# Router on un-normalised sums, narrow projection first, and subtractions moved to VectorE in a one-core encoder block

## The chip, the core and the metric

The kernel runs on one core of a Trainium2 chip. The metric is the device time of one execution in microseconds; less is better. The engines are named as in the profile: PE (TensorE matmuls), PEld (its weight loads), DVE (VectorE), ACT (ScalarE), POOL (GpSimd), SP (SyncE, which here issues most DMAs).

## What is computed

One encoder block over 256 tokens of width 1024, in float32. The parts that matter here:

```python
h @ w_in   # columns: [A: q | c_kv | q_idx | k_idx | w_idx] [B: q | k | v] [gate_A | gate_B]
# mixer A: the indexer's scores choose 64 keys of each query, then latent attention over them
# mixer B: chunked attention with a learned relative bias
m = sigmoid(gate_A) * (y_A @ Wa) + sigmoid(gate_B) * (y_B @ Wb); out = m @ w_out
x = LN(alpha * x + out)                 # ln1: (x - mean) * rstd * g + b
x = LN(alpha * x + MoE(x))              # top-4 of 32 experts of width 1024

def moe_ffn(x, w_router, b_router, ...):
    logits = (xf @ w_router + b_router).astype(jnp.float32)
    top_val, top_idx = lax.top_k(logits, TOP_K)
    gates = jax.nn.softmax(top_val, axis=-1)
    # each of the 32 experts: clamped SwiGLU of its tokens, weights of 3 x 1024 x 1024
```

## The kernel before, in words

All weights are read once. They pass through a pool of 27 SBUF slots of 1 MB (128 x 2048 float32). `load_next` (L85) issues the next weight load on SP's queue as soon as it is called in program order; the load then waits in that queue until the slot that it gets is released by its last reader. `pump(reserve)` issues loads until only `reserve` slots are unpromised; the table `RESERVE` gives the number for each call, and `used()` frees two slots and pumps.

**Mixer.** The tokens (xT, transposed, 256 KB per 256 features) are multiplied by w_in. To get float32 accuracy from a faster matmul form, a 1 MB chunk of weights is split into a rounded half `hi` (ACT, L178) and the rest `lo` = chunk − hi (L183, two subtractions of 128x1024), and three products hi·x_hi, hi·x_lo, lo·x_hi are summed (the tuple `THREE`). `LO_ENGINE` gives for each of 24 chunks the engine of the subtraction, V for DVE and G for POOL; `AHEAD` says how many chunks are split ahead of use. `LO_MERGED` gives the engine of the same subtraction for the merged branches.

PE's order is: index query projection (L244 in plain float32 for three of eight k, L247 split), narrow projection `g0` (L253: index keys, latent, index weights), then eight projections T0 to T7 of 512 columns (`project_T`, L282, and `project(5)`, L267), with small attention steps between: `ktr` (L347, transposes of index key and latent), `kat` (L373), `va` (L377), index scores, scores of mixers B and A. `maxima`, `exps`, `normalise` (L423, DVE) and `turn` (L446: 24 PE transposes of the probabilities `biasB` for mixer B, `sa` for A) and `attend` make each attention. After project(5) comes turn(sB), then T6, attend(vb), T7, turn(sA). Then the branches (L528), the output projection w_out (`out_chunk`, four quarters of the contraction for two token blocks) with the residual in `x1`.

**Norm and router.** `norm_apply` writes z = (x1 − mean)·rstd and x1 = z·g + b on DVE; `turn_z` transposes z, `route_sums` multiplies by the router weights scaled with ln1's gain, `route` picks the four experts, `count_up` and `one_hot` give each expert's row numbers, and `gather` (L651) multiplies x1 by the one-hot matrix so that the rows of the first two experts stand together. Small bf16 matmuls without use (`warm`, L226) stand between the steps.

**Experts.** 32 experts of 12 loads of 1 MB follow: gate and up (L775, L777), down (L809), summed back by L821. The last of them ends the program.

Of the kernel before, what the change touches and what calls it, by code (L numbers as in the profile page):

```python
# [50 lines left out]
def body(nc, tc, slots, sm, psp, xT_d, x_d, w_g0, w_qi, w_in, ikgb_d, wuk_d,  # L51
# [197 lines left out]
    free(6)  # L249
    g0ps = [bank("g0ps") for _ in range(NT)]  # L250
    for k in range(KD):
        for tb in range(NT):
            PE.matmul(g0ps[tb][:, 0:200], xT[:, k, tb * 128:(tb + 1) * 128], g0[:, k, :],  # L253
                      start=(k == 0), stop=(k == KD - 1))
    free(2)
# [113 lines left out]
    for j2 in range(2):  # L369
        p = bank("kat")  # L370
        for jj in range(2):
            j = 2 * j2 + jj
            PE.matmul(p[:, jj * 256:(jj + 1) * 256], wuk[:, j * 128:(j + 1) * 128], ckT, start=True, stop=True)  # L373
        acopy(kaT[:, 2 * j2:2 * j2 + 2, :], p.rearrange("p (j t) -> p j t", j=2))
# [189 lines left out]
    def norm_apply(tb, groups):  # L564

        m, dst = lnmv[:, tb, :], x1[:, tb, :]
# [3 lines left out]
        hs = [slice(i * 512, (i + 1) * 512) for i in range(2)]  # L570
        for cs in hs:
            V.tensor_scalar(z[:, cs], dst[:, cs], m[:, 0:1], m[:, 3:4], op0=ALU.subtract, op1=ALU.mult)
        for cs in hs:
            V.scalar_tensor_tensor(dst[:, cs], dst[:, cs], m[:, 0:1], ln1[0][:, cs], op0=ALU.subtract, op1=ALU.mult)
        for cs in hs:
            V.scalar_tensor_tensor(dst[:, cs], dst[:, cs], m[:, 3:4], ln1[1][:, cs], op0=ALU.mult, op1=ALU.add)
# [11 lines left out]
    def turn_z():  # L588
        for h in range(2):
            p = bank("rtr")  # L590
            for i in range(4):
                k = 4 * h + i
                PE.transpose(p[:, i * 128:(i + 1) * 128], z[:, k * 128:(k + 1) * 128], ident)
            acopy(zT[:, 4 * h:4 * h + 4, :], p.rearrange("p (k t) -> p k t", k=4))
# [3 lines left out]
    def router_row():  # L598
        p = bank("rrow")
        for k in range(KD):  # L600
            PE.matmul(p[0:1, 0:NE], lnc[:, 1, k:k + 1], wr[:, k, :], start=(k == 0), stop=(k == KD - 1))
        V.tensor_tensor(rrow, rrow, p[0:1, 0:NE], op=ALU.add)

    def route_sums(copy=vcopy):
# [8 lines left out]
    def route(tb):

        p = bank("rt")[:, 0:NE]
        PE.matmul(p, ones, rrow, start=True, stop=False)
        PE.matmul(p, rsum, eye4, start=False, stop=True)
        acopy(lg[:, tb, :], p)
        V.max(v8[:, tb, :], p)
# [1 line left out]
        V.match_replace(gt[:, tb, :], v8[:, tb, :], p, LOW)
        V.tensor_tensor(selb[:, tb, :], gt[:, tb, :], p, op=ALU.not_equal)
# [105 lines left out]
    norm_apply(1, 4)
    gather(P[:, 0].rearrange("p e s -> p (e s)"), 128, 0, gps)
    turn_z()  # L730
    route_sums(acopy)
    warm(6)
# [366 lines left out]
```

## Time and profile before

| | |
|---|---|
| device time, median of 3 runs | 1137.94 us (1136.99 to 1138.29) |
| device time of the profiled execution | 1137.62 us |
| span of the profiled execution | 1136.0 us |
| busy in the span: PE, DVE, ACT, POOL | 1061.2, 293.4, 228.7, 96.6 us |
| DMA over the span | 437.52 MB, mean 385 GB/s |

The span is what the trace covers; 1.6 us of the device time lie around it. A busy PE is not PE at its peak. The profiled execution lies 0.3 us under the median.

### The profile page before, as it was taken

The page shows a single profiled execution, that of the slowest core. Times are in us where ns is not written, and L with a number is a line of the kernel's source. Part 1 is how long each engine was busy: PE and PEld are TensorE (multiplying, and loading weights), DVE is VectorE, ACT ScalarE, POOL GpSimd, SP SyncE. Part 2 cuts the span into 40 slices and gives each one's busy share as a digit, 9 for nine tenths or more (in the row PEclk, how much of TensorE's full clock was granted, in tenths as well). Part 3 has the DMA queues.
Part 4 walks back from the last instruction along what each step waited for, and adds up shares of the span by engine and source line. Part 5 has one row for each costly group of instructions (what it writes and reads, how often), then busy time and mean ns, then how long its engine had stood idle before and what let it go on. Part 6 is the DMA issues. An engine that isn't in the chain of part 4 may idle for free. (4 is left out here: it accounts for less than half of the span.)

```text
span 1136.0 us, 13723 instructions
## 1 busy us (share of the span) xinstructions
PE 1061.2 (93%) x5599; PEld 535.3 (47%) x5599; DVE 293.4 (26%) x711; ACT 228.7 (20%) x425; POOL 96.6 (9%) x54
## 2 busy tenths in 40 slices
PE   8998999999999999999999988996999999989985
PEld 8997998543434343434343434342434343333432
DVE  5398556322111111111111111111021102011123
ACT  3557542211111111201111101111111111011112
POOL 4675232000000000000000000000000000000001
PEclk9999999999999999999999999998999999998998
DMA  9925477999999999999999999999999999999994
GB/s 361 419 108 221 149 267 293 404 399 420 421 421 421 422 420 421 420 422 421 420 422 421 421 421 421 421 421 419 421 421 421 422 421 421 421 407 421 421 419 173
DMA packets 63932, 437.52 MB, mean 385 GB/s; under 512 B 7252, under 2 KB 7892, under 8 KB 11892
## 3 DMA queue, kind: packets, MB, share of 16 engines
q1 hardware_dynamic: 62998, 434.20, 92.9%
q10 hardware_dynamic: 864, 2.36, 0.6%
q8 instruction: 47, 0.77, 0.3%
q14 instruction: 23, 0.19, 0.0%
HBM read 435.48 MB, written 1.05 MB: 384 GB/s over the span
## 5 line engine op out<-in xcount | busy, mean ns | idle before, releaser
L777 PE MATMUL gu<-ld,wa 128*64 128x512 f32 x1024 | 460.1, 602 | 28.9 <-DMA ld<-in_dram 28.9
L775 PE MATMUL gu<-ld,wa 128*64 128x512 f32 x1024 | 458.9, 601 | 7.0 <-PEq L851 3.8
L809 PE MATMUL y<-ld,wc 128*64 128x512 f32 x992 | 239.2, 596 | 16.3 <-DMA ld<-in_dram 16.3
L775 PEld LDWEIGHTS gu<-ld,wa 128*64 128x64 f32 x1024 | 135.8, 138 | 226.5 <-issue 219.7
L796 DVE TENSOR_TENSOR wc<-tr,wb 128x256 f32<-128x256 f32 x64 | 27.0, 421 | 706.6 <-PE tr L792 706.6
L777 PEld LDWEIGHTS gu<-ld,wa 128*64 128x64 f32 x1024 | 135.2, 138 | 112.7 <-DMA ld<-in_dram 60.3
L809 PEld LDWEIGHTS y<-ld,wc 128*64 128x64 f32 x992 | 77.0, 136 | 164.6 <-issue 122.2
L178 ACT ACTIVATE wb<-gu 128x512 f32<-128x512 f32 x64 | 38.2, 597 | 445.1 <-PE gu L775 232.9
L178 ACT ACTIVATE wc<-y 64x512 f32<-64x512 f32 (+1 forms) x66 | 38.2, 578 | 224.2 <-PE y L809 216.7
L183 POOL TENSOR_TENSOR lo<-ld,hi 128x1024 fp32r<-128x1024 f32 x30 | 76.5, 2575 | 62.6 <-ACT hi L178 50.3
L984 POOL PARTITION_BROADCAST ln<-ln x1 | 2.3, 2298 | 929.0 <-DMA ld<-in_dram 929.0
L651 PEld LDWEIGHTS ga<-wa,x 128*128 128x128 f32 x512 | 61.6, 196 | 12.3 <-issue 12.2
L651 PE MATMUL ga<-wa,x 128*128 128x128 f32 x512 | 64.8, 285 | 0.0
L282 PE MATMUL fm<-xh,hi 128*128 128x256 f32 x224 | 64.3, 287 | 0.0
L282 PE MATMUL fm<-xl,hi 128*128 128x256 f32 x224 | 63.4, 283 | 0.0
L282 PE MATMUL fm<-xh,lo 128*128 128x256 f32 x224 | 63.4, 283 | 0.0
L821 PE MATMUL sum<-wc,wb 128*128 128x512 f32 x120 | 54.0, 592 | 0.0
L178 ACT ACTIVATE hi<-ld 128x1024 fp32r<-128x1024 f32 x48 | 47.5, 1048 | 26.8 <-PE fm L282 12.3
L282 PEld LDWEIGHTS fm<-xh,hi 128*128 128x128 f32 x224 | 42.9, 192 | 0.7 <-issue 0.4
L282 PEld LDWEIGHTS fm<-xl,hi 128*128 128x128 f32 x224 | 43.0, 192 | 0.2 <-issue 0.2
L282 PEld LDWEIGHTS fm<-xh,lo 128*128 128x128 f32 x224 | 43.0, 192 | 0.0
L798 ACT ACTIVATE wa<-wc 128x256 f32<-128x256 f32 x64 | 26.6, 416 | 79.4 <-DVE wc L797 78.8
(235 smaller groups left out, 828.6 us busy)
## 6 DMA issues: line engine op xcount, KB each, us to landing
ld<-in_dram SPq DMA_DIRECT2D x404, 1024.0 KB, 19.8
ld<-in_dram SPq DMA_DIRECT2D x8, 512.0 KB, 13.7
wq<-in_dram ACTq DMA_DIRECT2D x3, 512.0 KB, 7.8
biasB<-in_dram SPq DMA_DIRECT2D x1, 1024.0 KB, 12.1
x<-in_dram SPq DMA_DIRECT2D x1, 1024.0 KB, 6.8
g<-in_dram SPq DMA_DIRECT2D x1, 800.0 KB
xT<-in_dram SPq DMA_DIRECT2D x3, 256.0 KB, 7.5
out_dram<-acc SPq DMA_DIRECT2D x3, 256.0 KB, 2.0
```

Of the source, the lines that this page charges most:

```text
L178: A.activation(o, i, AF.Copy)
L183: sub.tensor_tensor(lo.bitcast(F32R), t, hi, op=ALU.subtract)
L282: PE.matmul(ps[j // 2][:, j % 2 * 256:j % 2 * 256 + 256], part(i, b, k, 4)[:, j * 128:(j + 1) * 128], xHL[a][:, 4 * c + k, :], start=(c + ...
L651: PE.matmul(ps[j // per][:, (j % per) * n:(j % per + 1) * n], x1_cols(tb, j), Pt, start=(tb == 0 and j % per == 0), stop=(tb == 1), skip_g ...
L775: PE.matmul(ps[n][0:64, :], xe(j), wg(j, cs), start=(j == 0), stop=(j == KD - 1), skip_group_check=True)
L777: PE.matmul(ps[n][64:128, :], xe(j), wu(j, cs), start=(j == 0), stop=(j == KD - 1), skip_group_check=True)
L796: V.tensor_tensor(gg, pv[:, :, 0, :], bg(js), op=ALU.add)
L798: A.activation(sg_, gg, AF.Sigmoid, scale=1.702)
L809: PE.matmul(p[64 * n:64 * n + 64, :], hT[:, j, :], wd(j, slice(n * 512, (n + 1) * 512)), start=(j == 0), stop=(j == KD - 1), skip_group_ch ...
L821: PE.matmul(sums[tb][n], lhsT, rhs, start=start, stop=stop, skip_group_check=True)
L984: G.partition_broadcast(ln2_s, ln2_s[0:1, :])
```

## The change

1. **Start.** The loads come in another order: xT on SP's queue and the narrow weights g0 on ACT's, then the index query's weights wq. PE does the narrow projection first, with DVE splitting xT meanwhile; the index query follows, its `lo` on DVE; `ktr` and `kat` move ahead of T0, the index scores follow T0 directly, and T1 moves behind the top-k selection.
2. **Subtractions.** `LO_ENGINE` has V for all chunks but 5, 6 and 7 (before: 9 V and 15 G); `LO_MERGED` has V for all four.
3. **Order of the mixer.** T6 stands ahead of turn(sB), and attend(vb) behind T7.
4. **Router.** The transposes are of x1 as the residual left it, and the logits are put right afterwards: (x1·W − mean·colsum(W))·rstd + row, where W is the router with ln1's gain. ACT applies mean and rstd to x1 (two activations per block). ln1's gain and offset are applied to the gathered rows (8 activations of 128x128), and to x1 itself by two DVE operations in expert 0, where the slot of ln1 is freed. Of 36 warm matmuls of this stage 12 stay, and the gather of the first block stands in four pieces between the steps of the second.
5. `RESERVE` has 1 in place of 3 at its second place and 3 in place of 2 at its fourteenth.

```diff
-LO_MERGED = "GVGV"
-RESERVE = (4, 3, 3, 3, 4, 5, 3, 3, 3, 1, 3, 3, 3, 2, 3, 1, 2, 4, 3, 1, 5, 1, 1, 1, 0)
+LO_MERGED = "VVVV"
+RESERVE = (4, 1, 3, 3, 4, 5, 3, 3, 3, 1, 3, 3, 3, 3, 3, 1, 2, 4, 3, 1, 5, 1, 1, 1, 0)
-LO_ENGINE = "GVVGGGGGGGGGGVGVGVGVGVVV"
+LO_ENGINE = "VVVVVGGGVVVVVVVVVVVVVVVV"
...
-    for k0, n in ((0, 1), (1, 1), (2, 2), (4, 2), (6, 2)):
+    for k0, n in ((0, 1), (1, 1), (2, 2), (4, 4)):
         SP.dma_start(xT[:, k0:k0 + n, :], xT_d[:, k0:k0 + n, :])
-        A.dma_start(wq[k0 // 4][:, k0 % 4:k0 % 4 + n, :], w_qi[:, k0:k0 + n, :])
-    SP.dma_start(g0, w_g0)
+    for k0, n in ((0, 2), (2, 6)):
+        A.dma_start(g0[:, k0:k0 + n, :], w_g0[:, k0:k0 + n, :])
+    for k0, n in ((0, 2), (2, 2), (4, 4)):
+        SP.dma_start(wq[k0 // 4][:, k0 % 4:k0 % 4 + n, :], w_qi[:, k0:k0 + n, :])
...
     exps(sA, 0)
+    project_T(6, gate_sink(1, 0))
     turn(sB, 1)
     free(2)
-    project_T(6, gate_sink(1, 0))
-    attend(vb, 1)
     normalise(sA, 0)
     project_T(7, gate_sink(1, 1))
     free(2)
+    attend(vb, 1)
     turn(sA, 0)
...
+    def norm_apply(tb):
+
+        m, dst = lnmv[:, tb, :], x1[:, tb, :]
+        for i in range(2):
+            cs = slice(i * 512, (i + 1) * 512)
+            A.activation(dst[:, cs], dst[:, cs], AF.Identity, bias=m[:, 4:5], scale=m[:, 3:4])
...
-        PE.matmul(p, ones, rrow, start=True, stop=False)
-        PE.matmul(p, rsum, eye4, start=False, stop=True)
-        acopy(lg[:, tb, :], p)
-        V.max(v8[:, tb, :], p)
+        PE.matmul(p, rsum, eye4, start=True, stop=True)
+        l, m = lg[:, tb, :], lnmv[:, tb, :]
+        V.scalar_tensor_tensor(l, wsum, m[:, 0:1], p, op0=ALU.mult, op1=ALU.add)
+        V.scalar_tensor_tensor(l, l, m[:, 3:4], rowb, op0=ALU.mult, op1=ALU.add)
+        V.max(v8[:, tb, :], l)
...
+    def gathered_z(ps, dst):
+
+        for j in range(KD):
+            A.activation(dst[:, j, :], ps[j // 4][:, j % 4 * 128:(j % 4 + 1) * 128], AF.Identity,
+                         bias=lnc[:, 1, j:j + 1], scale=lnc[:, 0, j:j + 1])
...
         if e == 0:
+            for gain, op in ((ln1[0], ALU.mult), (ln1[1], ALU.add)):
+                V.tensor_tensor(x1, x1, gain[:, None, :].to_broadcast([128, NT, D]), op=op)
+            free()
             open_work()
```

Three places show what the new order does to the queues. First PE at the start, before (the last index query matmuls, then g0 and T0, whose rows are `fm`):

```order
L247 MATMUL qi<-xl,wqh_145 128x256
L247 MATMUL qi<-xh,wql_147 128x256
L253 MATMUL g0ps<-g_69,xT 128x200 x16
L282 MATMUL fm<-xh,hi 128x256
L282 MATMUL fm<-xl,hi 128x256
```

The same place after:

```order
L255 MATMUL qi<-xl,wqh_143 128x256
L255 MATMUL qi<-xh,wql_145 128x256
L341 MATMUL ktr<-ident,kidxT_ckvT 128x128 x4
L359 MATMUL kat<-kidxT_ckvT,uku 128x256 x4
L284 MATMUL fm<-xh,hi 128x256
L284 MATMUL fm<-xl,hi 128x256
```

The narrow projection is gone from between index query and T0 (it stands at the head), and ktr and kat are there instead. Second, DVE around the division of B's probabilities (`biasB`) by their sums, before:

```order
L183 TENSOR_TENSOR lo<-ld,hi 128x1024 x2
L421 RECIPROCAL sums<-sums 128x16
L423 TENSOR_TENSOR biasB_663<-biasB_663,sums 128x1024
L423 TENSOR_TENSOR biasB_664<-biasB_664,sums 128x2048
L175 COPY pt_1205<-ptr 128x512 x2
```

And after:

```order
L185 TENSOR_TENSOR lo<-ld,hi 128x1024 x4
L423 RECIPROCAL sums<-sums 128x16
L425 TENSOR_TENSOR biasB_553<-biasB_553,sums 128x1024
L425 TENSOR_TENSOR biasB_554<-biasB_554,sums 128x2048
L185 TENSOR_TENSOR lo<-ld,hi 128x1024 x4
L177 COPY pt_1319<-ptr 128x512 x2
```

Two more subtractions stand ahead of the division, and four between it and the copies of the transposed probabilities (`pt`). Third, SP's queue around the output projection and the router, with the semaphores that each load waits for, before:

```order
L85 DMA ld<-in_dram 128x2048 [waits DMAHW4_49,PE_49]
L85 DMA ld<-in_dram 128x2048 [waits DMAHW5_49,PE_49]
L85 DMA ld<-in_dram 128x2048 [waits DMAHW6_49,PE_49]
L85 DMA ld<-in_dram 128x2048 [waits DMAHW7_49,PE_49]
L85 DMA ld<-in_dram 128x2048 [waits DMAHW0_49,Pool_49]
L85 DMA ld<-in_dram 128x2048 [waits DMAHW1_49,PE_49]
L85 DMA ld<-in_dram 128x2048 [waits DMAHW2_49]
L85 DMA ld<-in_dram 128x2048 [waits DVE_49,DMAHW3_49,PE_49,Activation_49]
L85 DMA ld<-in_dram 128x2048 [waits DMAHW4_49,DVE_49,Pool_49]
L899 DMA wb<-in_dram 128x256 [waits DMAHW5_49,PE_49]
```

And after (`wb` is a small load of biases of the first experts):

```order
L85 DMA ld<-in_dram 128x2048 [waits DMAHW6_49]
L85 DMA ld<-in_dram 128x2048 [waits DMAHW7_49,PE_49]
L85 DMA ld<-in_dram 128x2048 [waits DMAHW0_49]
L85 DMA ld<-in_dram 128x2048 [waits DMAHW1_49,PE_49,Activation_49]
L922 DMA wb<-in_dram 128x256 [waits DMAHW2_49,PE_49]
L923 DMA wb<-in_dram 128x256 [waits DMAHW3_49]
L85 DMA ld<-in_dram 128x2048 [waits DMAHW4_49,PE_49]
L85 DMA ld<-in_dram 128x2048 [waits DMAHW5_49,DVE_49,Pool_49]
```

The load that takes the slot of ln1 (the one that waits for DVE and POOL) stood ahead of wb and now stands behind it, since the slot is freed in expert 0.

## Rows read from the trace of the kernel before

**Rows 1.** Stretches: length; busy of PE, PEld, DVE, ACT, POOL; granted clock; DMA; GB/s.

```profile
0.00:6.50 6.50, 4.56 (x34) 4.16 (x35) 1.60 (x8) 0.00 (x0) 1.21 (x8) 1.00 0.65 169
16.30:19.70 3.40, 3.40 (x19) 3.40 (x18) 0.00 (x0) 2.77 (x4) 2.60 (x3) 0.50 1.01 422
57.40:109.40 52.00, 51.99 (x402) 48.31 (x400) 45.49 (x95) 29.93 (x59) 33.34 (x13) 1.00 0.45 176
109.40:119.40 10.00, 4.30 (x25) 3.97 (x25) 8.15 (x5) 8.28 (x35) 4.09 (x2) 0.66 0.00 0
148.00:174.10 26.10, 26.10 (x244) 25.80 (x243) 17.35 (x24) 11.02 (x12) 6.55 (x3) 1.00 0.78 302
174.10:197.20 23.10, 23.10 (x150) 19.42 (x148) 14.48 (x24) 4.82 (x8) 4.04 (x2) 1.00 0.75 288
209.90:232.00 22.10, 22.10 (x99) 8.36 (x100) 5.14 (x21) 5.83 (x9) 0.00 (x0) 1.00 1.00 410
232.00:239.00 7.00, 7.00 (x34) 2.30 (x32) 1.37 (x6) 0.00 (x0) 0.00 (x0) 1.00 0.90 321
239.00:1119.40 880.40, 826.75 (x3868) 336.45 (x3864) 145.76 (x432) 123.54 (x235) 2.30 (x1) 0.99 1.01 419
```

**Rows 2.** Waits of SP's queue in 0 to 300 us (total, times, longest).

```profile
SPq L899 <- PE gu L777: 7.6, 1, 7.6
```

**Rows 3.** PE's timeline, start (start, duration, instruction, count, idle before and its releaser).

```profile
15.33 0.39 PE L247 MATMUL qi<-xh,wql 128*128 128x256 f32 x1 [0.99 <-POOL wql L183]
22.43 5.58 PE L253 MATMUL g0ps<-g,xT 128*128 128x200 f32 x32
27.70 0.42 PE L282 MATMUL fm<-xh,hi 128*128 128x256 f32 x1
39.36 0.60 PE L347 MATMUL ktr<-ident,kidxT_ckvT 128*128 128x128 f32 x4
54.21 1.99 PE L373 MATMUL kat<-kidxT_ckvT,uku 128*128 128x256 f32 x8
56.04 1.88 PE L377 MATMUL va<-uku,kidxT_ckvT 128*128 128x512 f32 x4
```

**Rows 4.** PE's timeline at the two turns.

```profile
111.56 0.79 PE L446 MATMUL ptr<-ident,biasB 128*128 128x128 f32 x4 [2.17 <-DVE biasB L423]
115.89 3.75 PE L446 MATMUL ptr<-ident,biasB 128*128 128x128 f32 x20 [3.54 <-DVE biasB L423]
119.39 0.36 PE L282 MATMUL fm<-xh,hi 128*128 128x256 f32 x1
145.46 0.60 PE L446 MATMUL ptr<-ident,sa_vb 128*128 128x128 f32 x4
148.00 0.36 PE L528 MATMUL br<-y,hi 128*128 128x256 f32 x1
```

**Rows 5.** DVE's timeline.

```profile
20.96 8.24 DVE L183 TENSOR_TENSOR lo<-ld,hi 128x1024 fp32r<-128x1024 f32 x4 [5.27 <-ACT hi L178]
40.00 0.55 DVE L348 TENSOR_SCALAR kidxT_ckvT<-ktr,ikgb 128x256 f32<-128x256 f32 x1 [4.76 <-PE ktr L347]
86.01 3.39 DVE L412 TENSOR_REDUCE mx<-biasB 128x8 f32<-128x1024 f32 x2
89.33 1.69 DVE L481 SCALAR_TENSOR_TENSOR sa_vb<-misc 128x128 f32<-128x128 f32 x8
90.94 2.76 DVE L481 SCALAR_TENSOR_TENSOR sa<-misc 128x256 f32<-128x256 f32 x8
105.59 2.36 DVE L183 TENSOR_TENSOR lo<-ld,hi 128x1024 fp32r<-128x1024 f32 x2 [2.00 <-issue]
108.15 7.48 DVE L423 TENSOR_TENSOR biasB<-biasB,sums 128x1024 f32<-128x1024 f32 x2
```

**Rows 6.** DVE's groups of L423 kept apart by shape (busy, mean ns).

```profile
L423 DVE TENSOR_TENSOR sa<-sa,sums 128x2048 f32<-128x2048 f32 x1 | 2.3, 2284 | 0.0
```

**Rows 7.** POOL's timeline beside the division.

```profile
107.53 5.96 POOL L183 TENSOR_TENSOR lo<-ld,hi 128x1024 fp32r<-128x1024 f32 x2 [9.26 <-ACT hi L178]
```

More of the change, by code (lines that the diff above doesn't have):

```diff
@@ L151, in body @@
     SP.dma_start(uku_s[:, 0:1024], wuk_d)
+    for _ in range(4):
+        load_next()
     wr = sm.tile([128, KD, NE], F32, name="wr")
@@ L233, in body @@
     wqHL = [[t.bitcast(F32R).rearrange("p (k c) -> p k c", k=4) for t in ts] for ts in (wqh, wql)]
+    g0ps = [bank("g0ps") for _ in range(NT)]
+    for k in range(KD):
+        for tb in range(NT):
+            PE.matmul(g0ps[tb][:, 0:200], xT[:, k, tb * 128:(tb + 1) * 128], g0[:, k, :],
+                      start=(k == 0), stop=(k == KD - 1))
+        sl = slice(k * 256, (k + 1) * 256)
+        split(xT_s[:, sl], xh_s[:, sl], xl_s[:, sl], vcopy, V)
+    free(1)
     qp = [bank("qi") for _ in range(4)]
     for k in range(KD):
-        sl = slice(k * 256, (k + 1) * 256)
-        split(xT_s[:, sl], xh_s[:, sl], xl_s[:, sl], vcopy, V)
+        sl = slice(k % 4 * 512, (k % 4 + 1) * 512)
         if k >= QI_NATIVE:
-            sl = slice(k % 4 * 512, (k % 4 + 1) * 512)
-            split(wq_s[k // 4][:, sl], wqh[k // 4][:, sl], wql[k // 4][:, sl])
+            split(wq_s[k // 4][:, sl], wqh[k // 4][:, sl], wql[k // 4][:, sl], sub=V)
         for j in range(4):
@@ L248, in body @@
                           start=False, stop=(k == KD - 1 and b == 1))
[L249 to L255, printed above, removed]
+    free(7)
     V.scalar_tensor_tensor(negd, negd, -1.0, negd, op0=ALU.mult, op1=ALU.min)
@@ L290, in copy_to @@
         return lambda js, p: acopy(dst[:, js, :], p)
-    ahead(AHEAD[0])
-    for j in range(4):
-        vcopy(qiT[:, j, :], qp[j][:, 0:256])
     kT_s = slot("kidxT_ckvT")
@@ L356, in relu_sink @@
         A.activation(rl[tb][:, heads[0]:heads[-1] + 1:2, :], ps, AF.Relu)
-    project_T(1, copy_to(kbT))
+    ahead(1)
+    for j in range(4):
+        (acopy if j % 2 else vcopy)(qiT[:, j, :], qp[j][:, 0:256])
+    for j2 in range(2):
+        p = bank("kat")
+        for jj in range(2):
+            j = 2 * j2 + jj
+            PE.matmul(p[:, jj * 256:(jj + 1) * 256], wuk[:, j * 128:(j + 1) * 128], ckT, start=True, stop=True)
+        acopy(kaT[:, 2 * j2:2 * j2 + 2, :], p.rearrange("p (j t) -> p j t", j=2))
+    qb_s = slot("qb")
+    qbT = qb_s[:, 0:1024].rearrange("p (j t) -> p j t", j=4)
+    kbT = qb_s[:, 1024:2048].rearrange("p (j t) -> p j t", j=4)
+    project_T(0, copy_to(qbT))
     for tb in range(NT):
@@ L368, in body @@
     va = uku_s[:, 1024:2048].rearrange("p (b c) -> p b c", b=2)
[L369 to L374, printed above, removed]
     for sb in range(NT):
@@ L397, in body @@
     SP.dma_start(b0_s[:, 0:1024], relb_d[:, 0:1024])
+    project_T(1, copy_to(kbT))
     project_T(2, copy_to(qaT))
@@ L504, in body @@
     mg = sg[0]
-    ones = sm.tile([1, 128], F32, name="ones")
+    ones = sm.tile([128, 128], F32, name="ones")
     V.memset(ones, 1.0)
@@ L508, in body @@
     V.tensor_tensor(wrg, wr, lnc[:, 0, :, None].to_broadcast([128, KD, NE]), op=ALU.mult)
+    V.tensor_tensor(wr, wr, lnc[:, 1, :, None].to_broadcast([128, KD, NE]), op=ALU.mult)
     eye4 = sm.tile([128, NE], F32, name="eye4")
@@ L562, in norm_stats, with norm_of @@
         V.bn_stats(lnst[:, tb, i, :], src[:, i * n:(i + 1) * n])
-    def norm_apply(tb, groups):
-        m, dst = lnmv[:, tb, :], x1[:, tb, :]
+    def norm_of(tb, groups):
+        m = lnmv[:, tb, :]
         V.bn_aggr(m[:, 0:2], lnst[:, tb, 0:groups])
@@ L569, in norm_apply @@
         V.reciprocal(m[:, 3:4], m[:, 2:3])
[L570 to L576, printed above, removed]
+        V.tensor_scalar(m[:, 4:5], m[:, 0:1], m[:, 3:4], -1.0, op0=ALU.mult, op1=ALU.mult)
+    def norm_apply(tb):
[3 more added lines that the diff above has]
+            A.activation(dst[:, cs], dst[:, cs], AF.Identity, bias=m[:, 4:5], scale=m[:, 3:4])
     lg = sm.tile([128, NT, NE], F32, name="lg")
@@ L586, in body, with turn, router_rows, route_sums @@
     cum = []
[L588 to L594, printed above, removed]
+    def turn(tb, js, copy=acopy):
+        p = bank("rtr")
+        n = len(js)
+        for i, j in enumerate(js):
+            PE.transpose(p[:, i * 128:(i + 1) * 128], x1_cols(tb, j), ident)
+        copy(xT1[:, tb, js[0]:js[0] + n, :], p[:, 0:n * 128].rearrange("p (k t) -> p k t", k=n))
     rsum = sm.tile([128, 128], F32, name="rsum")
-    def router_row():
+    def router_rows():
         p = bank("rrow")
[L600 to L604, printed above, removed]
+        PE.matmul(p[:, 0:2 * NE], ones, rows2, start=True, stop=False, skip_group_check=True)
+        PE.matmul(p[:, NE:2 * NE], ones[0:1, :], rrow, start=False, stop=True, skip_group_check=True)
+        V.tensor_scalar(wsum, p[:, 0:NE], -1.0, None, op0=ALU.mult)
+        vcopy(rowb, p[:, NE:2 * NE])
+    def route_sums(tb, copy=vcopy):
         p = bank("rt")
@@ L608, in route_sums @@
             g = k % 4
-            PE.matmul(p[32 * g:32 * g + 32, 0:128], wrg[:, k, :], zT[:, k, :], start=(k < 4), stop=(k >= 4),
+            PE.matmul(p[32 * g:32 * g + 32, 0:128], wrg[:, k, :], xT1[:, tb, k, :], start=(k < 4), stop=(k >= 4),
                       skip_group_check=True)
@@ L615, in route @@
         p = bank("rt")[:, 0:NE]
[L616 to L619 removed]
+        PE.matmul(p, rsum, eye4, start=True, stop=True)
[3 more added lines that the diff above has]
+        V.max(v8[:, tb, :], l)
         V.memset(v8[:, tb, 4:8], -LOW)
[L621 to L622 removed]
+        V.match_replace(gt[:, tb, :], v8[:, tb, :], l, LOW)
+        V.tensor_tensor(selb[:, tb, :], gt[:, tb, :], l, op=ALU.not_equal)
     def count_up(tb):
@@ L638, in body @@
     identa = wa_s[:, 1792:1920]
+    wsum, rowb, rows2 = wa_s[:, 1920:1952], wa_s[:, 1952:1984], wa_s[:, 1984:2048]
+    for i, w in enumerate((wrg, wr)):
+        V.tensor_reduce(rows2[:, i * NE:(i + 1) * NE], w.rearrange("p k e -> p e k"), axis=AX.X, op=ALU.add)
     def x1_cols(tb, j):
@@ L702, in body @@
     zz_s = slot("z")
-    z = zz_s[:, 0:1024]
-    zT = zz_s[:, 1024:2048].rearrange("p (k t) -> p k t", k=KD)
-    norm_apply(0, 2)
+    xT1 = zz_s.rearrange("p (b k t) -> p b k t", b=NT, k=KD)
+    norm_of(0, 2)
     out_chunk(1, 1)
@@ L708, in body @@
     out_chunk(2, 1, (0,))
+    turn(0, range(0, 4))
     out_chunk(3, 1, (0,))
-    router_row()
-    turn_z()
+    turn(0, range(4, 8))
+    router_rows()
+    norm_apply(0)
     norm_stats(x1[:, 1, :], 1, 0, 256)
@@ L715, in body @@
     out_chunk(2, 1, (1,))
-    route_sums(acopy)
+    route_sums(0, acopy)
     out_chunk(2, 1, (2,))
@@ L719, in body @@
     route(0)
+    turn(1, range(0, 4))
     out_chunk(3, 1, (1,))
@@ L724, in body @@
     out_chunk(3, 1, (2,))
+    turn(1, range(4, 6))
+    P0, P1 = [P[:, tb].rearrange("p e s -> p (e s)") for tb in range(NT)]
+    gather(P0, 128, 0, gps, (0, 1))
+    turn(1, range(6, 8))
     norm_stats(x1[:, 1, :], 1, 3, 256)
@@ L727, in body @@
     free(2)
[L728 to L732, printed above, removed]
+    norm_of(1, 4)
+    gather(P0, 128, 0, gps, (2, 3))
+    route_sums(1)
+    norm_apply(1)
+    gather(P0, 128, 0, gps, (4, 5))
     route(1)
-    free(2)
-    warm(20)
+    free(1)
+    gather(P0, 128, 0, gps, (6, 7))
+    warm(8)
     count_up(1)
-    warm(10)
+    warm(4)
     one_hot(0, 1, cum[1])
+    gather(P1, 128, 1, gps)
+    gathered_z(gps, xg_rows(0, KD))
     for tb in range(NT):
-        acopy(pos[:, tb, :], cum[tb])
-    gather(P[:, 1].rearrange("p e s -> p (e s)"), 128, 1, gps)
-    gathered(gps, 128, xg_rows)
+        vcopy(pos[:, tb, :], cum[tb])
     pump(next(pumps))
@@ L1061 @@
     bias = lambda b: b.reshape(NE, 4, 128, 2).transpose(2, 0, 1, 3).reshape(128, NE, KD)
+    pairs = lambda w: w.reshape(4, 128, 2, -1).transpose(1, 0, 2, 3).reshape(128, KD, -1)
     arrs = [
@@ L1075 @@
         np.concatenate([a["ln1_g"][0], a["ln1_b"][0]])[None, :],
-        np.stack([a["ln1_g"][0].reshape(KD, 128).T, a["ln1_b"][0].reshape(KD, 128).T], axis=1),
-        a["w_router"][0].reshape(KD, 128, NE).transpose(1, 0, 2),
+        np.stack([pairs(a["ln1_g"][0])[:, :, 0], pairs(a["ln1_b"][0])[:, :, 0]], axis=1),
+        pairs(a["w_router"][0]),
         a["b_router"],
```

6 lines of the change are left out of this document (removed).

## The prediction

> **What bounds the kernel now.** I read the table of stretches first [rows 1], because one average over the span mixes two regimes. From 239 us to 1119 us the DMA share is 1.01 at 419 GB/s: the experts wait for weights, and nothing that PE, DVE or ACT save there is worth anything. The stretch 209.90 to 232.00 is full too (1.00). Ahead of that the share is 0.45 (57 to 109 us), 0.00 (109 to 119 us), 0.78 and 0.75: the loads stand still because the 27 slots are full and are released only as PE works through the mixer. PE is busy 52.0 of 52.0, 26.1 of 26.1 and 23.1 of 23.1 us in these stretches, so up to about 200 us the kernel is bound by PE's order, and behind it by the bytes still to come. The link is what the sum below uses: when PE reaches the output projection x us sooner, the loads restart x us sooner, run without a pause, and the end comes x us sooner.
>
> The exception in PE's part is 109.40 to 119.40: PE is busy 4.30 of 10.00 us, and its granted clock falls to 0.66. PE's own timeline names the cause [rows 4]: the transposes of B's probabilities wait 2.17 us and 3.54 us for the division on DVE. The second look was PE's start [rows 3]: waits for a subtraction (0.99 us on POOL), and the clock at 0.50, which is 1.2 GHz, from 16.3 to 19.7 us [rows 1]. Last came SP's queue [rows 2], where one load waits 7.6 us for expert 1's matmuls, and DMA drops to 321 GB/s in 232 to 239 us [rows 1].
>
> **The change part by part.** Costs are of the profiled execution (1137.62 us), 0.3 us under the median.
>
> *The turn of B.* What must happen between the end of project(5) at 109.40 and T6 at 119.39 is 24 transposes. The same 24 for mixer A, whose operand is ready, go from 145.46 to 148.00 [rows 4]: 2.54 us. The rest, 10.00 − 2.54 = 7.46 us, is wait and half clock. With T6 in front, PE has 11.7 us of work (T0, of the same shape, takes 27.70 to 39.36 [rows 3]) while DVE divides. In the time of before, the division must then end by 109.4 + 11.7 = 121.1 us; it ended at 108.15 + 7.48 = 115.6 [rows 5].
>
> But DVE gets more to do ahead of it, so I count its row of work from the maxima of B at 86.01: maxima 3.39, the start of A's scores 1.69 + 2.76 [rows 5], four subtractions at 2.36/2 = 1.18 us (a pair takes 2.36 [rows 5]) 4.7, the additions of A's scores taken as long as their start 4.45, maxima of A 3.4, four subtractions 4.7, the two divisions 2.28 for the large one [rows 6] and half of it for the small one, 3.4. Sum 28.5: the end is at 114.5, 6.6 us ahead of need. The divisions are taken at 2.28 us and not at the 7.48 of before because POOL subtracted just then, 5.96 us for two [rows 7], and after the change it doesn't. If the eight subtractions cost the most that a DVE row shows, 8.24/4 = 2.06 us [rows 5], 7.0 us come on top and PE would wait 0.4 us. So +7.4 gained, bounds 5.7 (the two waits alone) to 7.46. What is late if this cover were gone is attend(vb), but it now stands behind T7, 11.7 us more.
>
> The four subtractions between the division and the copies of the turned probabilities [DVE's order in the change] take 4.7 us; 114.5 + 4.7 = 119.2, still ahead of 121.1.
>
> *The start.* Loads: 169 GB/s in the first 6.50 us [rows 1] are 1.10 MB, then 0.42 MB per us. xT and g0, 1.05 + 0.82 = 1.87 MB, are in at 8.3 us; wq, 2.10 MB more, at 13.4 us. The narrow projection takes 27.70 − 22.43 = 5.27 us for 16 matmuls [rows 3], 0.33 each. Four can run on the first quarter of g0, and twelve from 8.3 on end at 12.3 us. The index query follows: 12 float32 matmuls of 128x256 at the rate of kat, (56.04 − 54.21)/4 = 0.46 us [rows 3], 5.5 us; 60 split ones at T0's rate, 11.66/96 = 0.12 us, 7.3 us; end 25.1. Then ktr 0.6, a wait for DVE to scale index key and latent, two of 0.55 us [rows 5], kat 1.83: T0 starts at 28.6. Before, T0 started at 27.70, with ktr and kat still to do: 27.70 + 0.6 + 1.83 = 30.1. Gain 1.5 us. New in it is that PE, after its first four narrow matmuls, waits for data until 8.3 us; before, the clock fell to half for 3.4 us behind two short waits, which cost 1.7 us of work. Whether it falls again the order cannot tell; I take half such a fall, −0.85, bounds 0 and two falls, −3.4. The subtractions of wq on DVE, five of half the width of the 1.18 us ones, are about 3 us in all, beside 5.5 us of float32 matmuls.
>
> The Trainium skill (TensorE: Matmul & The Clock Gate, "Part 1: The HAM clock gate") has the slow clock as the default state that activity lifts; this agrees with the 0.50 behind PE's early waits, and speaks for a fall here, where PE waits for data.
>
> *Subtractions in the branches and the output projection.* In 148.0 to 197.2 us DVE is busy 17.35 + 14.48 = 31.8 of 49.2 us, and POOL does five operations there [rows 1]. As DVE subtractions these five cost 5 × 1.18 = 5.9 at most, to 37.7 of 49.2: nothing on the path, bound −1.0 for the last chunk, which PE needs at once. Covered by PE's 49.2 us.
>
> *Router.* In the stage from 197 to 210 us the new chain is shorter by DVE's four passes over x1 and four over z, but the first expert waits for nothing of it that sets the end: DMA is full from then on [rows 1], so the gain is 0, bound +3.0. The eight activations of the gathered rows and the two DVE passes over x1 in expert 0 (twice 2048 columns, each like the 2.28 us row [rows 6], some 4.6 us, at most double) lie beside gate and up matmuls.
>
> *SP's queue.* One load that now stands ahead of the biases moves behind expert 0: 1.05 MB less are in when the stage ends, 1.05/0.419 = 2.5 us [rows 1], −2.5. In return the experts start sooner against the stream, and the load's 7.6 us wait for expert 1 [rows 2], which cost (419 − 321)/419 × 7.0 = 1.6 us of DMA [rows 1], goes: +1.6. Together −0.9, bounds −2.5 and +1.6.
>
> Sum: 7.4 + 1.5 − 0.85 − 0.9 = 7.15 us. 1137.62 − 7.15 = 1130.5 for the profile; against the median 1137.94, **1130.8 us**.
>
> A rule of the Trainium skill (SBUF — State Buffer, "SBUF: two separate sides") says that DVE and GpSimd share a port pair as an exclusive lock: an operation of DVE with two SBUF inputs and one of GpSimd don't run together, and one waits the whole other out. The trace agrees: the large division took 4.4 us beside POOL and a like one 2.28 without (7.48 against 3.4 for both). By the rule the six halves left on POOL can each hold up DVE; that is the third rival.
>
> **The rivals.**
> 1. *The start gives back its gain.* The clock falls twice, or g0 comes late on ACT's queue. For it: 0.50 behind waits of 1 us; against: the same bytes come first. Gain 7.15 + 0.85 − 3.4 = 4.6: 1133.3 us.
> 2. *Router and queue count too.* The removed chain brings the loads forward by the 3.0 us bound and no load is lost (+0.9). Against: full DMA. Gain 11.0: 1126.9 us.
> 3. *POOL's chunks 5 to 7 hold DVE.* Six halves of up to 5.96/2 = 2.98 us [rows 7], 17.9 us in all; where DVE has slack it hides, but the first needed chunk behind them comes late by some 2 us (DVE is busy 45.5 of 52.0 us in 57 to 109 [rows 1]). Gain 5.1: 1132.8 us.
> 4. *The turn still waits.* The change doesn't do what it says: the division comes late behind the added subtractions and the 10 us stretch stays as it is, its idle time only moved behind T6. Against: 6.6 us of slack. Gain 7.15 − 7.4 = −0.2: 1138.1 us.
> 5. *Slower: a DVE subtraction costs what POOL's does.* The 14 subtractions that are counted on DVE ahead of the division (eight above, six earlier) cost 2.98 us rather than 1.18 [rows 5, 7]: 25.2 us more, less 6.6 of slack, 18.6 of wait in front of turn(sB). Then 7.15 − 18.6: 11.4 slower, 1149.4 us. It decides from (6.6 + 7.15 + 2.3)/14 = 1.15 more each, 2.33 us, on; the highest DVE row is 2.06.
>
> **How the numbers follow.** Chances: forecast 0.57, rival 1 0.15, rival 2 0.11, rival 3 0.08, rival 4 0.05, rival 5 0.04. 0.2% of this kernel, 2.3 us, is about what a measurement of it can tell from no change. Faster: forecast and rivals 1 to 3, 0.91; same: rival 4, 0.05; slower: rival 5, 0.04. The range runs from rival 2 less 0.4 us to rival 1 and 0.9 us of lost cover (the wait of 0.4 and half the bound of the last chunk), 1126.5 to 1134.2; left out are rivals 4 and 5 and the tails of the others.
>
> **What would show it.** In the changed profile: T0 starts near 28.6 us with ktr and kat behind it; no wait of PE for the division, and the clock at 1.00 from 110 to 120 us (if not, the first term fails); the branches start 8 us sooner, near 140; the first gate and up matmuls come some 10 us sooner than 209.9; no DMA dip near 232, and the rate from 240 on again 419 GB/s. Wrong it would be by waits of PE for `lo` in T4 to T7 (rivals 3, 5), a half clock ahead of T0 (rival 1), or a DMA share under 1 between 190 and 240 us.

## The result and the profile after

The changed kernel takes 1129.16 us (median of 4 runs, 1128.58 to 1130.15) against 1138.08 us of the kernel before beside it (the three executions of the table and one more): ratio 0.9924, 95% interval [0.9907, 0.9942], 8.9 us faster. The forecast was 1130.8 us. The profiled execution has a span of 1127.0 us (before 1136.0) and took 1128.58 us.

Stretches of the changed kernel, with the columns of [rows 1]: length, busy of PE, PEld, DVE, ACT and POOL, granted clock, DMA share, GB/s.

```profile
12.00:20.00 8.00, 8.00 (x49) 7.38 (x49) 4.64 (x14) 3.79 (x10) 0.00 (x0) 1.00 1.01 414
109.40:119.40 10.00, 10.00 (x86) 10.00 (x86) 5.76 (x6) 9.98 (x30) 0.00 (x0) 1.00 0.24 84
185.00:187.50 2.50, 2.50 (x32) 2.12 (x32) 0.95 (x4) 2.00 (x4) 0.00 (x0) 1.00 0.03 13
187.50:190.00 2.50, 2.25 (x21) 2.14 (x20) 2.01 (x10) 0.60 (x1) 0.00 (x0) 1.00 0.57 151
190.00:240.00 50.00, 49.26 (x273) 22.77 (x273) 15.27 (x48) 13.26 (x26) 0.00 (x0) 1.00 1.01 421
239.00:1110.00 871.00, 815.50 (x3805) 333.62 (x3803) 145.28 (x430) 120.80 (x229) 2.30 (x1) 1.00 1.01 419
```

The stretch 109.40 to 119.40, in which PE was busy 4.30 us at a clock of 0.66, is full at 1.00. The last pause of the loads is at 185 to 190 us; behind it DMA is full, the dip at 232 us of [rows 1] is gone, and the rate of the experts is the same 419 GB/s.

PE's timeline at the places of [rows 3] and [rows 4]: kat and T0 (`fm`) at the start, T6 right behind project(5), turn(sB) (`ptr<-ident,biasB`), the first branch matmul, and the first gate and up matmul.

```profile
26.05 1.97 PE L359 MATMUL kat<-kidxT_ckvT,uku 128*128 128x256 f32 x8 [1.08 <-issue]
27.66 0.47 PE L284 MATMUL fm<-xh,hi 128*128 128x256 f32 x1
...
107.08 0.28 PE L284 MATMUL fm<-xh,hi 128*128 128x256 f32 x1
...
118.59 2.78 PE L448 MATMUL ptr<-ident,biasB 128*128 128x128 f32 x24
...
138.18 0.48 PE L531 MATMUL br<-y,hi 128*128 128x256 f32 x2
...
197.37 0.64 PE L798 MATMUL gu<-ld,wa 128*64 128x512 f32 x1
```

The 24 transposes of B now stand in one group with no wait in front. T0 starts where it started before, but ktr and kat are already done. The branches start at 138.18 in place of 148.00: 9.8 us sooner. DVE's timeline at the division, beside [rows 5]:

```profile
103.39 4.63 DVE L185 TENSOR_TENSOR lo<-ld,hi 128x1024 fp32r<-128x1024 f32 x4 [0.71 <-ACT hi L180]
...
108.21 3.43 DVE L425 TENSOR_TENSOR biasB<-biasB,sums 128x1024 f32<-128x1024 f32 x2
```

The division ends at 111.64, 7 us ahead of turn(sB), and takes 3.43 us in place of 7.48. All that PE waits for up to the experts, but for 1.9 us at the very start (total, times, longest):

```profile
PE kat L359 <- issue: 1.1, 1, 1.1
PE cum L635 <- DVE selb L629: 0.8, 2, 0.5
PE ga L661 <- DVE wa L655: 0.2, 1, 0.2
```

On SP's queue the wait of [rows 2], now at L922, has not gone:

```profile
SPq L922 <- PE gu L800: 8.3, 1, 8.3
```

### The profile page after: what moved, and what is told of

Same layout as the page of the kernel before. It is cut to its first block, busy times and chain, and to the rows that moved or that the text cites. A ratio compares the mean times of both kernels' runs of the same rounds, so it can differ in the third digit from the quotient of the medians.

```text
span 1127.0 us, 13627 instructions
## 1 busy us (share of the span) xinstructions
PE 1056.5 (94%) x5559; PEld 533.8 (47%) x5559; DVE 311.3 (28%) x743; ACT 233.1 (21%) x433; POOL 25.4 (2%) x23
## 3 DMA queue, kind: packets, MB, share of 16 engines
HBM read 435.48 MB, written 1.05 MB: 387 GB/s over the span
## 4 chain that ended last, share of the span: by engine, by line
DMA 67%; PE 31%; DVE 1%; issue 0%; SPq 0%; DVEq 0%
DMA ld<-in_dram 66%; PE gu L798 8%; PE fm L284 7%; PE y L832 3%; PE br L531 2%; PE wo L681 2%; PE ga L661 1%; PE tm L269 1%; PE sum L844 1%; PE sce L331 1%; PE tr L815 1%; PE gu L800 1%; PE qi L255 1%; PE pv L464 0%; DMA xT<-in_dram 0%; PE ptr L448 0%
## 5 line engine op out<-in xcount | busy, mean ns | idle before, releaser
L832 PE MATMUL y<-ld,wc 128*64 128x512 f32 x992 | 242.9, 597 | 18.4 <-DMA ld<-in_dram 18.4
L185 DVE TENSOR_TENSOR lo<-ld,hi 128x1024 fp32r<-128x1024 f32 x42 | 50.4, 1258 | 6.6 <-ACT hi L180 6.6
L815 PEld LDWEIGHTS tr<-ident,wb 128*128 128x128 f32 x256 | 33.3, 208 | 13.7 <-issue 12.6
```

What stands on the lines that cost most here:

```text
L815: PE.transpose(p[:, i * 128:(i + 1) * 128], gu[:, (j // 2) * 256 + j % 2:(j // 2) * 256 + 256:2], ident)
L832: PE.matmul(p[64 * n:64 * n + 64, :], hT[:, j, :], wd(j, slice(n * 512, (n + 1) * 512)), start=(j == 0), stop=(j == KD - 1), skip_group_ch ...
```

## The experiments

Each run is timed beside the kernel before on the same chip, in five rounds. That kernel's median was 1137.37 us beside the order alone, the order undone, the subtractions undone and the start alone; 1137.71 beside the two router runs, one slot less and ln1 late; 1138.51 beside the waits filled and both slots late; and 1137.43 beside start and order. Gains over the kernel before are against that median; the recorded ratio with its 95% interval is not exactly the quotient of the two medians. A difference between two changed kernels is that of their own medians. Taken as the difference of their gains it comes out up to 1.1 us otherwise, and both are given where that matters.

**Order alone.** The kernel before with two lines moved, T6 forward and attend(vb) back:

```diff
+    project_T(6, gate_sink(1, 0))
     turn(sB, 1)
     free(2)
-    project_T(6, gate_sink(1, 0))
-    attend(vb, 1)
     normalise(sA, 0)
     project_T(7, gate_sink(1, 1))
     free(2)
+    attend(vb, 1)
     turn(sA, 0)
```

> The kernel before with only the new order of the mixer (T6 ahead of turn(sB), attend(vb) behind T7). Theory, the forecast's first term: the division ends near 115.6 us, T6 covers it, PE waits for it no more, the clock stays at 1.00, and the whole 7.4 us reach the end: 1130.7 us. Rival, the order helps only together with the subtractions on DVE: POOL still doubles the division, PE waits again in front of turn(sB) or the loads come free no sooner; gain under 3 us, over 1135 us.

Measured 1129.83 us, ratio 0.9931 [0.9918, 0.9945]: 7.5 us faster, what the theory gave. Its DVE and POOL timelines at the division:

```profile
107.25 7.57 DVE L423 TENSOR_TENSOR biasB<-biasB,sums 128x1024 f32<-128x1024 f32 x2
```

```profile
106.64 6.03 POOL L183 TENSOR_TENSOR lo<-ld,hi 128x1024 fp32r<-128x1024 f32 x2 [8.98 <-ACT hi L178]
```

The division is as slow as before, beside POOL's two subtractions, and it no longer matters: it ends at 114.8, and PE's timeline has turn(sB) in one group behind T6:

```profile
119.85 2.79 PE L446 MATMUL ptr<-ident,biasB 128*128 128x128 f32 x24
```

**Order undone.** The changed kernel with the same lines moved back.

> The changed kernel with the old order of the mixer (turn(sB), T6, attend(vb), T7). Its division stands at 108.21 to 111.64 us, project(5) ends at 107.1. Theory: PE waits for the first part until about 109.4 and for the second until 111.6, so that T6 starts some 4.1 us later than with cover, and up to 1.7 us more by a half clock: 1133.3 to 1135 us. Rival: the order alone was worth the same 7.4 us here as before: 1136.6 us.

Measured 1136.20 us, ratio 0.9985 [0.9976, 0.9994]: 7.0 us slower than the changed kernel. The rival's number was right. PE's timeline there:

```profile
109.72 0.63 PE L448 MATMUL ptr<-ident,biasB 128*128 128x128 f32 x4 [2.45 <-DVE biasB L425]
111.91 4.50 PE L448 MATMUL ptr<-ident,biasB 128*128 128x128 f32 x20 [1.57 <-DVE biasB L425]
116.07 0.56 PE L284 MATMUL fm<-xh,hi 128*128 128x256 f32 x1
```

The waits are 4.0 us, as the theory had them, but the 20 transposes take 4.50 us where 2.78 us do for 24. The stretch from project(5) to T6 shows the clock:

```profile
107.10:116.07 8.97, 4.95 (x26) 4.61 (x25) 6.51 (x7) 8.55 (x35) 0.00 (x0) 0.68 0.06 8
```

Of these 9.0 us, 2.54 would be the transposes without a wait, so 6.4 us are lost. The theory had counted too little beside the waits; the next run settles what it was.

**The waits filled.** Order undone, with small matmuls without use in the two waits:

```diff
             for bi, (tb, sb) in enumerate(((0, 0), (1, 0), (1, 1))):
+                if w == 1 and j2 == 0 and bi < 2:
+                    warm((32, 20)[bi])
                 p = bank("ptr")
```

> The changed kernel with the old order of the mixer (1136.2 us) and small matmuls without use (32 and 20 of 128x128 bf16) in PE's two waits for the division. In the run without them PE goes from project(5) at 107.1 to T6 at 116.07 us, 9.0 us, of which 4.0 are waits and 2.54 the transposes. Theory: the other 2.4 us are the clock at 0.50; with the waits filled the clock stays at 1.00, T6 starts at 113.7 and the end is 2.4 us sooner, 1133.8 us. Rival: the 2.4 us are the reading of the transposes' operands or copies behind them, not the clock; within 0.5 us of 1136.2 or later by the added matmuls.

Measured 1133.48 us, 2.7 us faster than with the waits empty (3.9 as the difference of the gains). PE's timeline and the same stretch:

```profile
109.48 0.63 PE L450 MATMUL ptr<-ident,biasB 128*128 128x128 f32 x4 [0.65 <-DVE biasB L425]
109.95 1.28 PE L228 MATMUL warm<-wt 128*128 128x128 bf16 x20
111.69 2.37 PE L450 MATMUL ptr<-ident,biasB 128*128 128x128 f32 x20 [0.46 <-DVE biasB L425]
113.82 0.36 PE L284 MATMUL fm<-xh,hi 128*128 128x256 f32 x1
```

```profile
107.10:113.82 6.72, 5.61 (x76) 5.31 (x73) 5.93 (x7) 6.72 (x30) 0.00 (x0) 1.00 0.01 2
```

T6 starts at 113.82 (expected 113.7) with the clock at 1.00 throughout, and the 20 transposes take 2.37 us in place of 4.50 with the same operands and the same copies behind them, so the rival falls. Of the 6.4 us that the order saves up to T6, 2.3 are the clock at 1.2 GHz (116.07 − 113.82) and the rest is waiting for the division. The rule of the Trainium skill (TensorE: Matmul & The Clock Gate, "Part 1: The HAM clock gate") that activity releases the throttle fits this row. With the waits empty T6 also begins at half clock. The first branch matmul shows the whole loss, in the order undone and then with the waits filled:

```profile
145.20 0.48 PE L531 MATMUL br<-y,hi 128*128 128x256 f32 x2
142.43 0.48 PE L533 MATMUL br<-y,hi 128*128 128x256 f32 x2
```

Against 138.18 in the changed kernel that is 7.0 us, as in the medians: 2.8 us of clock and 4.2 of waiting. The two moved lines were not tried one by one.

**Subtractions undone.** The changed kernel with the old engines:

```diff
-LO_MERGED = "VVVV"
+LO_MERGED = "GVGV"
-LO_ENGINE = "VVVVVGGGVVVVVVVVVVVVVVVV"
+LO_ENGINE = "GVVGGGGGGGGGGVGVGVGVGVVV"
```

> The changed kernel with LO_ENGINE and LO_MERGED as before (15 of 24 chunks subtracted on POOL). Theory, the forecast's zero for this part: the division is again twice as long but ends before T6 does, PE waits nowhere for it; change within 1 us of 1129.2. Rival: POOL's subtractions and the lock with DVE put chunks late for PE; more than 2.3 us slower, over 1131.5 us, with PE waits for lo in T1 to T7 or the branches.

Measured 1128.81 us, ratio 0.9925 [0.9911, 0.9938], not to be told from the changed kernel's 1129.16. The division, in DVE's timeline, is slow again, and is covered:

```profile
106.22 7.57 DVE L425 TENSOR_TENSOR biasB<-biasB,sums 128x1024 f32<-128x1024 f32 x2
```

It ends at 113.8, 5.0 us ahead of turn(sB) at 118.8. So 12 of the 24 chunks and two of the four merged branches, moved from one engine to the other, are worth nothing that shows.

**Start alone.** The kernel before with the changed start, up to T1 behind the selection (item 1 of the change, and the second entry of RESERVE).

> The kernel before with only the new start (load order, narrow projection first, split of the index weights on DVE, ktr and kat ahead of T0, T1 behind the selection, second entry of RESERVE 1). Theory: PE is ahead by what the changed kernel shows at T0, 30.1 - 27.7 = 2.4 us, and the end comes 2.4 us sooner: 1135.7 us. Rival: the lead is eaten by the wait for the division, whose time is set by DVE and POOL and not by PE: PE waits longer at turn(sB), gain under 0.5 us, 1137.6 us or more.

Measured 1136.92 us, ratio 0.9996 [0.9987, 1.0005]: a gain of 0.4 us that cannot be told from none. The number is the rival's, but not by its mechanism. PE reaches the end of project(5) at 107.3 us (108.4 with the router alone, whose start and mixer are those of before) and waits as long as before for the division:

```profile
109.61 0.63 PE L448 MATMUL ptr<-ident,biasB 128*128 128x128 f32 x4 [2.14 <-DVE biasB L425]
113.97 4.50 PE L448 MATMUL ptr<-ident,biasB 128*128 128x128 f32 x20 [3.73 <-DVE biasB L425]
```

The lead of 1.1 us passes through the waits; in T6, which starts at half clock in both, 0.3 us of it go, and the branches start at 147.39, 0.7 us ahead of the run with the router alone.

A second reading explains why 2.4 us was too much to expect. The profiled execution of the kernel before had the clock at half in its start, but the runs with the order alone and the router alone, with that very start, had not. Stretches of before and then of the router alone:

```profile
12.00:20.00 8.00, 6.30 (x38) 5.89 (x37) 3.58 (x8) 4.22 (x7) 5.35 (x4) 0.79 1.02 420
```

```profile
12.00:20.00 8.00, 5.95 (x45) 5.34 (x44) 4.74 (x8) 4.36 (x7) 5.20 (x5) 1.00 1.02 426
```

With the order alone and with the router alone T0 starts at 26.8 us and not at 27.70. So 0.9 of the 2.4 us was in one execution's clock, not in the order.

**Start and order.**

> The kernel before with the new start and the new order of the mixer (subtractions and router as before; fourteenth entry of RESERVE as before). The order alone gave 1129.8, the start alone 1136.9 (0.5 us sooner). Theory: without cover the start's lead is lost in the half clock behind PE's wait for the division; with cover it shows, and gives the 1.3 us by which the branches of the changed kernel lead those with the order alone (138.2 and 139.4 us), up to the 1.9 us of the run with the old router: 1128 to 1128.5 us. Rival: the start is worth only the 0.5 us that it gives alone, 1129.3 us or more, and the rest comes from the subtractions on DVE.

Measured 1128.83 us (1127.70 to 1129.96), ratio 0.9921 [0.9906, 0.9935]: 8.6 us faster, 1.0 us more than the order alone (1129.83). That lies between theory and rival and the intervals overlap, so this run doesn't tell them apart. It was profiled in its slowest execution, in which the last 28 matmul rows of the narrow projection took 6.87 us (5.08 in the run with the router undone), at full clock, so that T0 starts at 29.55 us:

```profile
7.19 6.87 PE L239 MATMUL g0ps<-g,xT 128*128 128x200 f32 x28 [0.51 <-DMA xT<-in_dram]
```

What makes it vary was not tried.

**Router undone.** The changed kernel with the norm, router and gather of before.

> The changed kernel with the old norm and router (z, ln1 applied by DVE ahead of the experts, slot of ln1 freed there, 36 warm matmuls); all else as changed. Theory, the forecast's queue term of -0.9 us and 0 for the router: the end comes up to 0.9 us sooner or at the same time, 1128.3 to 1129.2 us. Rival, the shorter chain brings the loads forward: in the changed kernel the loads run without a pause from about 188 us, in the kernel before only from 200 us, which is 2.3 us more than PE's lead of 9.7 us: 2 to 3 us slower, 1131 to 1132 us.

Measured 1127.94 us, ratio 0.9915 [0.9902, 0.9929]: 1.2 us faster than the changed kernel by the medians, 0.9 as the difference of the gains, near the theory's 0.9. The intervals of the two kernels overlap, so the size is loose. The first three stretches are of this run, the last is of the changed kernel:

```profile
0.00:190.00 190.00, 186.08 (x1480) 175.40 (x1480) 143.07 (x251) 93.85 (x169) 20.65 (x20) 1.00 0.71 273
185.00:187.50 2.50, 2.50 (x32) 1.99 (x30) 0.21 (x1) 1.00 (x3) 0.00 (x0) 1.00 0.88 370
190.00:240.00 50.00, 49.26 (x282) 22.10 (x281) 12.98 (x45) 10.39 (x21) 0.00 (x0) 1.00 1.00 405
0.00:190.00 190.00, 186.67 (x1470) 176.21 (x1471) 141.50 (x252) 95.75 (x171) 20.22 (x20) 1.00 0.70 268
```

With the old router about 1 MB more, one load, is in at 190 us (273 against 268 GB/s), worth 2.4 us at 419 GB/s, and 0.8 MB less come in the next 50 us (405 against 421 GB/s), worth 1.9 us. The additional load runs at 185 to 187.5 us, where the changed kernel's DMA stands still (13 GB/s). The slot of ln1 doesn't make this difference: both kernels hold it through that pause. Why one slot comes free later with the new router was not tried.

**Router alone**, the opposite edit:

> The kernel before with only the new norm and router (gain and offset at the gathered rows and in expert 0). Theory: no gain, 1138 to 1139 us. Rival, the shorter chain counts: 2 to 3 us faster, 1135 to 1136 us.

Measured 1138.22 us, ratio 1.0004 [0.9995, 1.0013]: no change. The shorter chain to the first expert brings nothing to the end, in neither kernel; in the changed one the expert's matmuls start at 197.37 us, 12.5 us sooner, while the branches lead by only 9.8.

**One slot less.** The changed kernel with `NSLOT = 26`.

> The changed kernel with 26 slots in place of 27. Theory, the link of the sum (the end is the last pause of the loads plus the bytes left): PE's time in the mixer stays, one load of 1.05 MB less is in at the last pause, 2.5 us slower: 1131.7 us. Rival: the loads are late only locally and the experts have slack; within 0.5 us of 1129.2.

Measured 1131.40 us, ratio 0.9947 [0.9933, 0.9960]: 2.2 us slower than the changed kernel (2.6 as the difference of the gains), near the 2.5 us of 1.05 MB. PE's waits are those of the changed kernel but for 0.2 us at the start.

**The slot of ln1 taken late.** In the changed kernel ln1's slot is held from 170 us on but first read in expert 0:

```diff
-        x1_s, ln1_s = slot("x1"), slot("ln1")
+        x1_s = slot("x1")
...
     free(2)
+    ln1_s = late_norm()        # slot, load and broadcast of ln1
+    ln1 = (ln1_s[:, 0:1024], ln1_s[:, 1024:2048])
     norm_of(1, 4)
...
-RESERVE = (4, 1, 3, 3, 4, 5, 3, 3, 3, 1, 3, 3, 3, 3, 3, 1, 2, 4, 3, 1, 5, 1, 1, 1, 0)
+RESERVE = (4, 1, 3, 3, 4, 5, 3, 3, 3, 1, 3, 3, 3, 3, 3, 1, 2, 4, 3, 1, 4, 1, 1, 1, 0)
```

> The changed kernel with the slot of ln1 taken and loaded only behind the last out projection (its first use is in expert 0), and one more weight load let ahead of x in its place. Theory: 1.05 MB more are in at the last pause of the loads, 2.5 us faster: 1126.7 us. Rival: DMA is full from 188 us on anyway and the extra load only moves another one behind it; within 0.5 us of 1129.2.

Measured 1126.64 us (1126.58 to 1127.25), ratio 0.9904 [0.9889, 0.9919]: 2.5 us faster than the changed kernel (2.2 as the difference of the gains), as the theory had it.

**Also the slot of wa late**, with the small rows of the router kept in tiles that are free by then:

> The changed kernel with the slot of ln1 taken late, as in the run that took 1126.6 us, and the slot of wa (one-hot rows, gathered tokens) taken behind out_chunk(2, 1) in place of ahead of the output projection, so that two more weight loads stand ahead of x. Theory: loads still pause near 180 to 188 us with ln1 late alone, so another 1.05 MB there is worth up to 2.5 us: 1124.1 us, and nothing waits for wa. Rival: the pause is filled from the wrong side, since the extra load's slot comes free only near 190 us or x comes late for the residual; within 0.5 us of 1126.6 or slower.

Measured 1125.92 us (1125.69 to 1126.51), ratio 0.9890 [0.9875, 0.9905]: another 0.7 us by the medians, 1.5 as the difference of the gains, not 2.5. Its stretches around the pause:

```profile
175.00:180.00 5.00, 5.00 (x27) 4.26 (x26) 2.13 (x4) 0.00 (x0) 0.00 (x0) 1.00 1.01 424
180.00:185.00 5.00, 5.00 (x32) 4.38 (x30) 1.81 (x5) 1.34 (x3) 0.00 (x0) 1.00 0.73 272
185.00:187.50 2.50, 2.50 (x32) 2.17 (x32) 0.95 (x4) 1.84 (x4) 0.00 (x0) 1.00 0.00 0
187.50:190.00 2.50, 2.25 (x20) 2.14 (x20) 2.15 (x10) 0.60 (x1) 0.00 (x0) 1.00 0.55 164
...
200.00:240.00 40.00, 40.00 (x192) 15.97 (x189) 9.16 (x30) 7.23 (x13) 0.00 (x0) 1.00 0.99 403
```

DMA is full to 180 us now, but 185.0 to 187.5 stays empty, and 200 to 240 us runs at 403 GB/s, where the kernel with ln1 late has 415 and the changed kernel 420: part of what is loaded early is lost again in the first experts. It is the fastest version here, 12.6 us under the kernel before.

The end follows what DMA has moved by 240 us, behind which it is full. These are one slot less, the changed kernel, ln1 late and both late:

```profile
0.00:240.00 240.00, 235.91 (x1740) 199.02 (x1741) 156.82 (x299) 109.00 (x197) 20.23 (x20) 1.00 0.75 295
0.00:240.00 240.00, 235.93 (x1741) 198.99 (x1742) 156.77 (x299) 109.00 (x197) 20.22 (x20) 1.00 0.76 300
0.00:240.00 240.00, 234.87 (x1743) 198.31 (x1744) 154.96 (x299) 109.02 (x198) 20.22 (x20) 1.00 0.78 303
0.00:240.00 240.00, 235.72 (x1743) 198.96 (x1744) 154.94 (x299) 108.99 (x197) 20.22 (x20) 1.00 0.77 305
```

The spans are 1129.4, 1127.0, 1125.1 and 1123.8 us. 1 GB/s over 240 us is 0.24 MB, or 0.57 us at 419 GB/s: from 295 to 305 that makes 5.7 us, and the spans differ by 5.6.

## Why the prediction was right, point by point

- **The turn of B, +7.4.** Right in mechanism and size. Alone it gives 7.5 us; undone in the changed kernel it costs 7.0 (7.8 as the difference of the gains). The division was put 5.1 us behind project(5)'s end (114.5 − 109.4) and ended 4.5 behind it. That POOL's absence would make it short was right (3.43 us), but nothing hung on it: with POOL there it takes 7.57 us and T6 covers it too. What the forecast took as one sum of wait and half clock is in the changed kernel 4.2 us of wait and 2.8 us of clock.
- **The start, +1.5 − 0.85.** The step that was mis-sized. The half fall of the clock that I took off did not come: 1.00 from 12 to 20 us, and T0 at 27.66. The 28.6 held no fall, so the working itself was 0.9 long: the narrow projection ends at 11.99 (12.3 expected), the twelve float32 matmuls take 4.99 us (5.5), and from ktr to T0 it is 3.29 us (3.5). Read from the profiled executions alone, the gain at T0 is 2.4 us (30.1 − 27.7), of which 0.9 is the fall in the start of one execution of the kernel before. Against a start without that fall the gain is 1.5 us, the forecast's number, but by luck: the fall in the old start and the length of the working cancel. With cover the start is worth 1.0 us by the medians, without it 0.4, neither clear of the intervals. Rival 1 (1133.3 us), clock falls in the new start, is refuted: the granted clock is 1.00 from 5 to 27 us in every profile with that start, and PE waits there for xT, at most 1.4 us, and not for g0.
- **Subtractions in the branches and the output projection, 0.** Right: 1128.81 with them undone, the difference inside the noise. The profile of the changed kernel refutes rivals 3 and 5: PE waits for no `lo`, and DVE's four subtractions ahead of the division took 4.63 us, 1.16 each, as counted. Rival 4 falls with the single group of 24 transposes without a wait.
- **Router 0, queue −0.9.** Right in sign and near in size, inside overlapping intervals: without the router part the changed kernel is 0.9 to 1.2 us faster. Its two halves show in the trace, about 2.4 us for a load less at the last pause and 1.9 us for the dips that go (−2.5 and +1.6 in the forecast). The reasons given don't hold. The missing load is not the one that now stands behind expert 0's biases, where DMA is full (1.01 from 190 us), but one that the old router lets through at 185 us, and why is open. And the wait of SP's queue for the first expert, which the forecast took for the cause of the dip, is still there (8.3 us for L922). The dip at 232 us went all the same, so the +1.6 is right by luck. What is shown is the link behind both: a slot less costs 2.2 us, the slot of ln1 given back at the pause gains 2.5. Rival 2 (1126.9 us) had the router's chain bring the loads forward; the run with the router undone refutes it.
- **The sum.** By the trace of the changed kernel: 9.8 us at the branches, 9.0 at the end of the span, so 0.8 lost between. The forecast had 8.05 and 0.9. The difference of 1.8 us at the branches is the start. The gain is not known as finely as that: beside the experiments the kernel before had medians of 1137.37 to 1138.51 us, which puts the changed kernel 8.2 to 9.4 us under it.

What stays open, beside the slot that the new router frees late: how much of the last microsecond between start and order (1128.83) and the router undone (1127.94), which differ by the subtractions and one entry of RESERVE, is real; their intervals overlap. The entry of RESERVE was not tried by itself.

## What to carry to other kernels

Where an engine stalls for another in a program that is bound by its order, look for a block of independent work that stands right behind the stall and put it in front: here two moved lines gave 7.5 us of the 8.9, and the much larger edits around them about 1 us each way or nothing that shows. Price such a stall with the clock that it takes down, not with its wait alone. Where weight loads end the program at a constant rate, the end is the last pause of the loads plus the bytes left, so a slot that is held through that pause without being read is worth up to one load, 2.5 us for 1 MB here. The next slot given back brought only 0.7 to 1.5 us, since DMA lost part of it again in the first experts.
